# First norm by rows, one root for rows 4 to 7, epsilon on VectorE, fillers on TensorE, and the recurrence put ahead in the scheduler

## The chip, the cores and the metric

One kernel runs on one core of a Trainium2 chip. The metric is the device time of one execution in microseconds (us). The profile gives the times of single instructions on the core's engines: PE (TensorE, matmuls and transposes), PEld (its weight loads), DVE (VectorE), ACT (ScalarE), POOL (GpSimd) and SP (which issues DMAs). "L213" is line 213 of the kernel before; in the rows of the changed kernel's order the line numbers are its own, and the text says which line of the kernel before each one was.

## What is computed

One layer of a decoder: RMSNorm, a gated linear recurrence with eight heads, a squared-ReLU MLP behind a second RMSNorm, and a last RMSNorm. All is float32, 1024 rows by 1024 columns. Cut to what matters here:

```python
def _rmsnorm(x, gain):
    y = x * lax.rsqrt(jnp.mean(x * x, axis=-1, keepdims=True) + NORM_EPS)
    return y * gain

h = _rmsnorm(x, norm_mix)              # the "first norm"
q, f, i, g = jnp.split(h @ w_in, 4, axis=-1)
# per head, over time:  S_t = diag(f_t) S_{t-1} + k_t v_t^T ;  o_t = S_t^T q_t
x = x + (norm(o) * out_norm * silu(g)) @ w_out
x = x + squared_relu_mlp(_rmsnorm(x, norm_mlp))
return _rmsnorm(x, norm_final)
```

## The kernel before

**Products.** A float32 product is made of three matmuls on operands that are split in two parts: `split_mm` (L210 to L213) issues high times high (L211), high times low (L212) and low times high (L213). A splitting is one ACT instruction for the high part and one DVE instruction for the low part: L171 and L172 for the weights `w0a`, `w0c` and so on, L114 and L115 for the sums `ht1` to `ht4`, L313 and L314 for the transposed rows `h0B...`. The first two products (`w0`, `w1`) go plainly, by `plain_pair`; from `w2` on, `pair` uses seven products in place of eight (a Strassen scheme), for which L324 and L334 keep values `R` of the transposed rows.

**First norm.** Eight tiles `x0` to `x7` of 128 rows each are loaded by SP. `stats_1` (L284) makes a row's mean of squares `ss`: on ACT (L290) for even tiles, on DVE (L288) for odd ones. `rstd_of` (L122) then has two POOL instructions: L124 adds epsilon, L125 raises to the power of -0.5. `norm_scale` (L192, DVE) multiplies the tile in place. `transposed` (L196) makes one PSUM bank of four 128x128 transposes (L199, PE), one from each of four row tiles, for one of the eight column blocks kb; so the first bank needs all four tiles. Before them L131 issues 60 transposes of the identity into a bank `warm` that nobody reads.

The first half (`x0` to `x3`) is done at the start. The second half (`x4` to `x7`) is done by a list `hooks`, one entry of which is called ahead of each block kb (three matmuls) of `plain_pair`: statistics, scales, then the banks `tr010` to `tr017` of the second half, each of them in every second entry.

**Recurrence.** For each head `scan_units` (L512) gives a list of units: `small`, `middle`, `leaf(16)`, `big(32)`, `big(64)`, `kt`, and so on, with `None` for an empty place. `pump` (L233) takes one place from the list each time that the projections of the next head have issued 1730 ns of matmuls by its own count (650 per block kb), so that the unit's PE work stands between those matmuls. Between the units stands the chain on DVE: `carry_q`, `carry_k`, `carry_f` (L361, L368, L374) multiply prefixes into `q`, `k`, `f`, for chunks of 1, 2, 4, up to 64; `middle` needs `qe` (L555), `big(32)` and `big(64)` need `q` and `k` after the carries of 16 and 32, `kt` (L624, transposes of `k`) needs the carry of 64, and L596 `tot` stands right behind that carry. `copy_predicated` (L539 to L582) takes the units' results out of PSUM.

**What sets the order.** PE's order is the order of the code, everywhere. Up to L734 (`in_order.close()`), that is until the first half of `w0` and `w1` is done, ACT, DVE and POOL follow the code as well; then a scheduler orders those engines by priorities, until the MLP, where the code's order holds again. All engines run their own queue in order: an instruction that waits holds up what stands behind it.

Of the kernel before, what the change touches and what calls it, by code (L numbers as in the profile page):

```python
# [29 lines left out]
P = 128  # L30
# [13 lines left out]
AHEAD = 6  # L44
WARM = 60


@with_exitstack
def trunk(ctx: ExitStack, tc: tile.TileContext, x, gains, masks, gfin, w_in, w_out, w1, w2, out):
# [72 lines left out]
    def rstd_of(ss, eps, width, tag):  # L122
        r = pool.tile([P, width], F32, name=f"rs_{tag}", tag=f"rs{width}", bufs=8 if width == 1 else 2)
        nc.gpsimd.tensor_scalar(r, ss, eps, None, op0=ALU.add)  # L124
        nc.gpsimd.tensor_tensor(r, r, neghalf[:, :width], ALU.pow)  # L125
        return r


    warm = psum.tile([P, 512], F32, name="warm", tag="d")
    for _ in range(WARM):  # L130
        nc.tensor.transpose(warm[:, :P], ident, ident)  # L131

# [62 lines left out]

    def transposed(which, half, kb, hn, place=None):  # L196
        ps = psum.tile([P, 4, P], F32, name=f"tr{which}{half}{kb}", tag="s")
        for j in range(4):
            nc.tensor.transpose(ps[:, j, :], hn[j][:, kb * P:(kb + 1) * P], ident)  # L199
        name = BLOCKS[half][kb // 4]  # L200
        t = hc[name, kb % 4] = hslot(half if place is None else place, kb, f"h{which}{name}{kb}")
        return ps.rearrange("p a b -> p (a b)"), gn[:, which, kb:kb + 1], t
# [13 lines left out]
    units = []  # L216
    owed = [0.0]
    spacing = [SPACING]

# [3 lines left out]
    def next_unit():  # L223

        u = units[0]
        if isinstance(u, tuple) and u not in complete:
            return False
        units.pop(0)
        if callable(u):
            u()  # L230
        return True
# [17 lines left out]
    with tc.tile_pool(name="scan", bufs=1) as sp:  # L249
# [12 lines left out]
        lb = pool.tile([P, 32], F32, name="lb")  # L262
        gneg, lb = lb[:, 8:16], lb[:, :8]
        lo = pool.tile([P, 8], F32, name="lbe")
# [19 lines left out]
        def stats_1(tb):  # L284

            ss = pool.tile([P, 1], F32, name=f"ss{tb}", tag="ss", bufs=8)
            if tb % 2:
                nc.vector.tensor_tensor_reduce(junk[1], xs[tb], xs[tb], 1.0 / D, 0.0, ALU.mult, ALU.add, ss)  # L288
            else:
                nc.scalar.activation(junk[0], xs[tb], AF.Square, scale=D ** -0.5, accum_out=ss)  # L290
            rs[tb] = rstd_of(ss, EPS, 1, f"n{tb}")

        for tb in range(4):
            stats_1(tb)
        for tb in range(4):
            norm_scale(xs[tb], xs[tb], rs[tb])
        ensure(1)
        nc.gpsimd.memset(Ac, 0.0)
# [10 lines left out]
        def transposes_1(half):  # L309

            def one(kb):
                flat, g, t = transposed(0, half, kb, xs[4 * half:4 * half + 4], 1 - half)
                nc.scalar.activation(t[:, 0], flat, AF.Copy, scale=g)  # L313
# [28 lines left out]
        def scale_1(tb):  # L342
# [4 lines left out]
        hooks += first  # L347
        hooks += [pieces(stats_1, 4, 5), pieces(stats_1, 6, 7), lambda: None, pieces(scale_1, 4, 5),
                  pieces(scale_1, 6, 7)] + [lambda: None] * 7
# [162 lines left out]
        def scan_units(h, tl):  # L512
# [168 lines left out]
            def zt():  # L681

                z = tl["sg"]
                for a in range(2):
# [9 lines left out]

            return (([None] * 5 + [small] + [None] * 3 if h == 0 else [None] * 3 + [small, None, None]) + [middle, None, leaf(16, 7)]
                    + [big(32), big(64), None, kt, ("values", h), vt, kv, None, o_unit, z_unit, None, zt])
# [49 lines left out]
        for h in range(1, NH):  # L746
            tl = heads[h] = {}
            pair(h, tl, 0)
            prefixes(tl)
            units.extend(scan_units(h, tl))  # L750
            if h == NH - 1:
                spacing[0] = LAST_SPACING
            pair(h, tl, 1)
            complete.add(("values", h))
# [437 lines left out]
```

## Time and profile before

| | |
|---|---|
| Time, median of 3 runs | 1164.58 us (1163.2 to 1167.33) |
| Time of the profiled execution | 1162.14 us |
| Its span from first to last instruction | 1160.4 us |
| Around the span | 1.74 us |
| Busy in the span, DVE | 792.7 us (68%) |
| Busy in the span, ACT | 576.3 us (50%) |
| Busy in the span, POOL | 47.6 us (4%) |
| HBM traffic over the span | 123 GB/s |

A row of the timeline reads: start in us from the span's start, length in us, engine, line, operation, output tile <- input tiles, shapes, number of instructions merged into the row, and in brackets how long the engine had stood idle before and what released it. A row of the windows view gives a stretch and its length, then for PE, PEld, DVE, ACT and POOL the busy time and the instructions, then the granted share of TensorE's clock, the DMA engines' share and GB/s. A row of the waits view reads: who waited for whom, us in total, how often, the longest.

### The profile page before, as it was taken

Reading aid. Unit: us, or ns where it says so; the run is one execution under the profiler, and the core shown is the slowest. Engines: PE = TensorE matmul, PEld = TensorE weight load, DVE = VectorE, ACT = ScalarE, POOL = GpSimd, SP = SyncE. Lnnn points to the kernel's source line nnn. Section 1 sums busy time; section 2 is a strip of 40 time slices with the busy share of each in tenths; the row PEclk is TensorE's granted clock in tenths of the full one; section 3 lists DMA queues with packets and bytes.
Section 4 is the critical chain, followed back from the end, with each engine's and each line's share of the span. In section 5 each row is a group of like instructions: output and inputs, shape, how many; then the busy total and the mean of one; then the engine's idle time right before and its main releaser. Section 6 shows DMA issues by size and latency. Waiting matters only on the chain.

```text
span 1160.4 us, 17548 instructions
## 1 busy us (share of the span) xinstructions
PE 1142.0 (98%) x7108; PEld 945.8 (82%) x7108; DVE 792.7 (68%) x1139; ACT 576.3 (50%) x1004; POOL 47.6 (4%) x78
## 2 busy tenths in 40 slices
PE   8999999999999999999999999999999999999997
PEld 7777788887878778888888888888888888888886
DVE  6896868778686876426856645665588756677673
ACT  6646455564645573237545454545453443323552
POOL 3100000000000000010000000000000000000011
PEclk9999999999999999999999999999999999999999
DMA  6111121111112175021245324532797545422331
GB/s 259 37 37 53 41 73 56 46 47 55 44 50 73 56 248 171 19 97 67 91 163 200 122 113 165 199 138 98 272 373 286 186 170 179 148 91 92 127 127 73
DMA packets 43139, 143.38 MB, mean 124 GB/s; under 512 B 4913, under 2 KB 5041, under 8 KB 43057
## 3 DMA queue, kind: packets, MB, share of 16 engines
q1 hardware_dynamic: 42192, 141.05, 34.1%
q8 instruction: 56, 0.92, 0.3%
q10 hardware_dynamic: 864, 1.20, 0.3%
q14 instruction: 27, 0.21, 0.1%
HBM read 100.81 MB, written 41.42 MB: 123 GB/s over the span
## 4 chain that ended last, share of the span: by engine, by line
PE 83%; DVE 12%; ACT 2%; POOL 1%; issue 1%; DMA 1%; POOLq 0%; DVEq 0%; ACTq 0%
PE m2X L213 5%; PE m2X L211 5%; PE m2X L212 5%; PE m1X L212 4%; PE m1X L211 4%; PE m1X L213 4%; PE pX L211 3%; PE pX L213 3%; PE pX L212 3%; PE m2Y L213 3%; PE m2Y L211 3%; PE m2Y L212 2%; PE op L211 2%; PE op L213 2%; PE op L212 2%; DVE k L368 2%
## 5 line engine op out<-in xcount | busy, mean ns | idle before, releaser
L993 ACT ACTIVATE a<-ai 128x1024 fp32r<-128x1024 f32 x56 | 59.0, 1054 | 72.0 <-PE m2X L212 23.6
L994 DVE TENSOR_TENSOR a<-ai,a 128x1024 fp32r<-128x1024 f32 x56 | 68.3, 1220 | 11.5 <-ACT a L993 11.5
L896 ACT ACTIVATE e<-e 128x1024 f32<-128x1024 f32 x21 | 22.3, 1063 | 67.3 <-DVE e L1027 67.3
L211 PE MATMUL op<-wo,zh 128*128 128x512 f32 x128 | 51.0, 398 | 0.0
L213 PE MATMUL op<-wo,zh 128*128 128x512 f32 x128 | 50.0, 391 | 0.0
L212 PE MATMUL op<-wo,zh 128*128 128x512 f32 x128 | 49.8, 389 | 0.0
L151 DVE TENSOR_TENSOR xr<-xr,op 128x512 f32<-128x512 f32 x24 | 16.4, 687 | 44.9 <-PE op L213 44.9
L1054 DVE TENSOR_TENSOR acc<-acc,m2X 128x512 f32<-128x512 f32 x32 | 21.1, 685 | 36.1 <-PE m2X L213 36.0
L361 DVE TENSOR_TENSOR q<-q,f 128x512 f32<-128x512 f32 x56 | 38.6, 689 | 2.0 <-PE lv L609 2.0
L368 DVE TENSOR_TENSOR k<-k,f 128x512 f32<-128x512 f32 x56 | 38.4, 686 | 0.0
L893 ACT ACTIVATE e<-e 128x1024 f32<-128x1024 f32 x32 | 34.0, 1062 | 1.0
L151 DVE TENSOR_TENSOR raw<-raw,raw 128x512 f32<-128x512 f32 x42 | 28.9, 689 | 0.7
L586 ACT ACTIVATE AT<-Ac 32x256 f32<-32x256 f32 x32 | 13.3, 416 | 30.6 <-DVE Ac L582 30.3
L213 PEld LDWEIGHTS op<-wo,zh 128*128 128x128 f32 x128 | 24.0, 188 | 5.2
L211 PEld LDWEIGHTS op<-wo,zh 128*128 128x128 f32 x128 | 24.0, 188 | 4.9
L212 PEld LDWEIGHTS op<-wo,zh 128*128 128x128 f32 x128 | 24.1, 188 | 4.7
L1015 ACT ACTIVATE e<-m1X 128x512 f32<-128x512 f32 x28 | 16.0, 593 | 19.8 <-PE m1X L213 19.8
L124 POOL TENSOR_SCALAR rs_f<-fs 128x1 f32<-128x1 f32 x4 | 2.1, 514 | 577.7 <-ACT ot L1058 577.7
L678 ACT ACTIVATE z<-o,rs_z 128x128 f32<-128x128 f32 x64 | 17.4, 384 | 16.4 <-POOL rs_z L125 16.4
L666 PE MATMUL o<-v,AT 128*128 128x128 f32 x128 | 23.4, 275 | 0.0
L668 PE MATMUL o<-S,q 128*128 128x128 f32 x112 | 21.7, 275 | 0.0
L1054 DVE TENSOR_TENSOR acc<-acc,m2Y 128x512 f32<-128x512 f32 x16 | 10.8, 687 | 15.4 <-PE m2Y L213 13.6
(1721 smaller groups left out, 3731.0 us busy)
## 6 DMA issues: line engine op xcount, KB each, us to landing
raw<-in_w_in SPq DMA_DIRECT2D x32, 512.0 KB, 3.6
ai<-adt SPq DMA_DIRECT2D x32, 512.0 KB, 4.5
adB<-e SPq DMA_DIRECT2D x24, 512.0 KB, 2.6
adt<-t SPq DMA_DIRECT2D x24, 512.0 KB, 4.3
ai<-adB SPq DMA_DIRECT2D x24, 512.0 KB, 4.6
x<-in_x SPq DMA_DIRECT2D x8, 512.0 KB, 7.3
iw<-in_w_out SPq DMA_DIRECT2D x16, 256.0 KB, 3.3
xr<-in_x SPq DMA_DIRECT2D x8, 512.0 KB, 8.2
```

What stands on the lines that cost most here:

```text
L151: nc.vector.tensor_tensor(out_, a, b, ALU.add)
L211: nc.tensor.matmul(ps, lhi, rhi, start=start, stop=False, **more)
L212: nc.tensor.matmul(ps, lhi, rlo, start=False, stop=False, **more)
L213: nc.tensor.matmul(ps, llo, rhi, start=False, stop=stop, **more)
L361: nc.vector.tensor_tensor(qo, qo, te.to_broadcast([P, n, m]), ALU.mult)
L368: nc.vector.tensor_tensor(ke, ke, to.to_broadcast([P, n, m]), ALU.mult)
L666: nc.tensor.matmul(ps[:, j, :], AT[:, c, :], v[:, c, :], start=True, stop=c == 0)
L893: nc.scalar.activation(t, t, AF.Square)
L896: nc.scalar.activation(t, t, AF.Relu, scale=sign)
L993: nc.scalar.activation(hi, x, AF.Copy)
L994: nc.vector.tensor_tensor(lo, x, hi.bitcast(F32), ALU.subtract)
L1054: nc.vector.tensor_tensor(t, t, ps, op)
```

## The change

It has four parts.

1. **Rows.** In the first half of the first norm, the statistics of all four tiles are on ACT. Each tile is scaled as soon as its root is there, and its four transposes go into four banks held open together (`first_banks`). The 60 transposes of the identity become 36 ahead of the first tile, and 6, 6, 6 and 4 behind the transposes of the four tiles.
2. **Epsilon and roots.** In the first norm epsilon is added on DVE. For tiles 4 to 7 the four `ss` stand in one 128x4 tile, so that one DVE addition and one POOL root do for all four. The other norms keep `rstd_of`.
3. **Hooks.** The root has an entry of its own in `hooks`, so all that follows stands one block kb later.
4. **Scheduler.** A unit is recorded with `tc.high_priority(150)`, and with 400 from the second product of the last head on. In the list of head 0 the unit `small` stands one place earlier and the units behind it two places earlier.

```diff
-WARM = 60
+WARM = 36
+WARM_ROW = (6, 6, 6, 4)
...
-    for _ in range(WARM):
-        nc.tensor.transpose(warm[:, :P], ident, ident)
+    def keep_warm(n):
+        for _ in range(n):
+            nc.tensor.transpose(warm[:, :P], ident, ident)
+
+    keep_warm(WARM)
...
+    ahead = [150]
...
         if callable(u):
-            u()
+            with tc.high_priority(ahead[0]):
+                u()
...
-        gneg, lb = lb[:, 8:16], lb[:, :8]
+        gneg, ss4, rs4, lb = lb[:, 8:16], lb[:, 16:20], lb[:, 20:24], lb[:, :8]
...
-            ss = pool.tile([P, 1], F32, name=f"ss{tb}", tag="ss", bufs=8)
-            if tb % 2:
+            ss = ss4[:, tb - 4:tb - 3] if tb >= 4 else pool.tile([P, 1], F32, name=f"ss{tb}", tag="ss", bufs=8)
+            if tb in (5, 7):
...
-            rs[tb] = rstd_of(ss, EPS, 1, f"n{tb}")
-
+            return ss
+
+        def rstd_1(r, ss):
+            nc.vector.tensor_scalar(r, ss, EPS, None, op0=ALU.add)
+            nc.gpsimd.tensor_tensor(r, r, neghalf[:, :r.shape[1]], ALU.pow)
+
+        first_banks = [transpose_bank(0, 0, kb) for kb in range(4)]
         for tb in range(4):
-            stats_1(tb)
-        for tb in range(4):
+            rs[tb] = pool.tile([P, 1], F32, name=f"rs{tb}", tag="rs1", bufs=8)
+            rstd_1(rs[tb], stats_1(tb))
             norm_scale(xs[tb], xs[tb], rs[tb])
+            for kb in range(4):
+                transpose_rows(first_banks[kb], xs, kb, (tb,))
+            keep_warm(WARM_ROW[tb])
...
-        hooks += [pieces(stats_1, 4, 5), pieces(stats_1, 6, 7), lambda: None, pieces(scale_1, 4, 5),
+
+        def rstd_second():
+            rstd_1(rs4, ss4)
+            for i in range(4):
+                rs[4 + i] = rs4[:, i:i + 1]
+
+        hooks += [pieces(stats_1, 4, 5), pieces(stats_1, 6, 7), lambda: None, rstd_second, pieces(scale_1, 4, 5),
...
-            return (([None] * 5 + [small] + [None] * 3 if h == 0 else [None] * 3 + [small, None, None]) + [middle, None, leaf(16, 7)]
+            return (([None] * 4 + [small] + [None] * 2 if h == 0 else [None] * 3 + [small, None, None]) + [middle, None, leaf(16, 7)]
...
             if h == NH - 1:
                 spacing[0] = LAST_SPACING
+                ahead[:] = [400]
```

`transpose_bank` and `transpose_rows` are the two halves of the old `transposed`: the bank, and the transposes of chosen row tiles into it.

**DVE's queue in the first half of the first norm**, before. `ss1` and `ss3` are sums of squares, `rs_n` the roots from POOL, `w0a` the low part of the first weight, `h0B110` the low part of the first transposed block:

```order
L288 ISA junk1_193,ss1_199<-x1_78 128x1024
L288 ISA ss1_199 128x1
L288 ISA junk1_193,ss3_209<-x3_80 128x1024
L288 ISA ss3_209 128x1
L192 TENSOR_SCALAR x0_77<-x0_77,rs_n0_196 128x1024
L192 TENSOR_SCALAR x1_78<-x1_78,rs_n1_201 128x1024
L192 TENSOR_SCALAR x2_79<-x2_79,rs_n2_206 128x1024
L192 TENSOR_SCALAR x3_80<-x3_80,rs_n3_211 128x1024
L172 TENSOR_TENSOR w0a_218<-raw00_163,w0a_218 128x128 x4
L314 SCALAR_TENSOR_TENSOR h0B110_234<-tr000_229,gn_73,h0B110_234 128x512
```

The same place of DVE's queue now (L308 adds epsilon, L197 is the old L192, L177 the old L172, L337 the old L314):

```order
L308 TENSOR_SCALAR rs0_174<-ss0_175 128x1
L197 TENSOR_SCALAR x0_77<-x0_77,rs0_174 128x1024
L308 TENSOR_SCALAR rs1_190<-ss1_191 128x1
L197 TENSOR_SCALAR x1_78<-x1_78,rs1_190 128x1024
L308 TENSOR_SCALAR rs2_206<-ss2_207 128x1
L197 TENSOR_SCALAR x2_79<-x2_79,rs2_206 128x1024
L308 TENSOR_SCALAR rs3_222<-ss3_223 128x1
L197 TENSOR_SCALAR x3_80<-x3_80,rs3_222 128x1024
L177 TENSOR_TENSOR w0a_236<-raw00_139,w0a_236 128x128 x4
L337 SCALAR_TENSOR_TENSOR h0B110_247<-tr000_170,gn_73,h0B110_247 128x512
```

Two statistics have left DVE, four additions of a 128x1 tile have come, and each scale stands directly behind its own addition, with POOL's root between the two.

**DVE's queue in the second half of the first norm**, before (`w1a`, `w1b` and `w1c` are low parts of weights, `qd0` is the first use of a finished product):

```order
L288 ISA junk1_193,ss5_343<-x5_82 128x1024
L288 ISA ss5_343 128x1
L288 ISA junk1_193,ss7_356<-x7_84 128x1024
L288 ISA ss7_356 128x1
L172 TENSOR_TENSOR w1a_367<-raw10_171,w1a_367 128x512
L192 TENSOR_SCALAR x4_81<-x4_81,rs_n4_340 128x1024
L192 TENSOR_SCALAR x5_82<-x5_82,rs_n5_345 128x1024
L192 TENSOR_SCALAR x6_83<-x6_83,rs_n6_353 128x1024
L192 TENSOR_SCALAR x7_84<-x7_84,rs_n7_358 128x1024
L397 SCALAR_TENSOR_TENSOR qd0_384<-qd0_384,qs_188,pp0000_253 128x16x32
L172 TENSOR_TENSOR w1b_396<-raw11_172,w1b_396 128x512
L314 SCALAR_TENSOR_TENSOR h0B120_419<-tr010_414,gn_73,h0B120_419 128x512
```

And now (L302 is the old L288, L116 the old L115; the sums of squares and roots lie in `lb`):

```order
L302 ISA junk1_169,lb_154<-x5_82 128x1024
L302 ISA lb_154 128x1
L116 TENSOR_TENSOR ht33_559<-R11_312,ht33_559 128x512
L302 ISA junk1_169,lb_154<-x7_84 128x1024
L302 ISA lb_154 128x1
L177 TENSOR_TENSOR w1a_349<-raw10_147,w1a_349 128x512
L308 TENSOR_SCALAR lb_154<-lb_154 128x4
L197 TENSOR_SCALAR x4_81<-x4_81,lb_154 128x1024
L197 TENSOR_SCALAR x5_82<-x5_82,lb_154 128x1024
L197 TENSOR_SCALAR x6_83<-x6_83,lb_154 128x1024
L197 TENSOR_SCALAR x7_84<-x7_84,lb_154 128x1024
L426 SCALAR_TENSOR_TENSOR qd0_368<-qd0_368,qs_164,pp0000_256 128x16x32
```

One addition of 128x4 stands ahead of the four scales, and the low part of `ht33`, which stood much later, has come in between the two statistics.

**DVE's queue at the end of head 0's recurrence**, before, from the carry of 16 to `tot` (`raw30` are sums of weights, `w3...` low parts of weights of the next product):

```order
L361 TENSOR_TENSOR q0_383<-q0_383,f0_403 128x32x16
L368 TENSOR_TENSOR k0_402<-k0_402,f0_403 128x32x16
L582 COPY_PREDICATED Ac_177<-mk_74,lv0_16_890 128x256
L374 TENSOR_TENSOR f0_403<-f0_403 128x32
L151 TENSOR_TENSOR raw30_467<-raw30_467,raw31_468 128x512
L361 TENSOR_TENSOR q0_383<-q0_383,f0_403 128x16x32
L368 TENSOR_TENSOR k0_402<-k0_402,f0_403 128x16x32
L172 TENSOR_TENSOR w3s3_1095<-raw30_467,w3s3_1095 128x512
L374 TENSOR_TENSOR f0_403<-f0_403 128x16
L172 TENSOR_TENSOR w3s1_1050<-raw30_467,w3s1_1050 128x512
L361 TENSOR_TENSOR q0_383<-q0_383,f0_403 128x8x64
L368 TENSOR_TENSOR k0_402<-k0_402,f0_403 128x8x64
```

And now, from the carry of 32 on (L390, L397 and L403 are the old L361, L368 and L374, L625 is `tot`, the old L596):

```order
L390 TENSOR_TENSOR q0_367<-q0_367,f0_387 128x16x32
L397 TENSOR_TENSOR k0_386<-k0_386,f0_387 128x16x32
L177 TENSOR_TENSOR w2d_894<-raw21_321,w2d_894 128x512
L403 TENSOR_TENSOR f0_387<-f0_387 128x16
L177 TENSOR_TENSOR w3a_968<-raw30_440,w3a_968 128x512
L390 TENSOR_TENSOR q0_367<-q0_367,f0_387 128x8x64
L397 TENSOR_TENSOR k0_386<-k0_386,f0_387 128x8x64
L625 TENSOR_TENSOR tot0_952<-f0_387 128x8
L177 TENSOR_TENSOR w2s4_891<-raw20_320,w2s4_891 128x512
L177 TENSOR_TENSOR w3b_1000<-raw31_441,w3b_1000 128x512
L156 TENSOR_TENSOR raw30_440<-raw30_440 128x512
L156 TENSOR_TENSOR raw30_440<-raw30_440,raw31_441 128x512
```

Six instructions of 128x512 that stood ahead of `tot` stand behind it now: `w2s4`, `w3b`, two sums `raw30`, `w3s3` and `w3s1`. On PE, `small` of head 0 stands three blocks kb (nine matmuls) earlier, and `kt` one block: the seven transposes of `kt` stood behind the three matmuls of `ht33` and stand ahead of them now. DVE's queue of heads 1 to 6 has not moved, nor has any DMA in SP's queue. ACT's has moved there in one thing: of the four copies L586 of a head, three now stand behind the four copies L612 of `big(32)`. In head 0 the copies L586 and L612 also stand ahead of the evacuation L479 of `pX2` behind `w2s2`, which stood ahead of them.

More of the change, by code (lines that the diff above doesn't have):

```diff
@@ L194, in trunk, with transpose_bank, transpose_rows, transposed @@
     BLOCKS = (("B11", "B21"), ("B12", "B22"))
-    def transposed(which, half, kb, hn, place=None):
-        ps = psum.tile([P, 4, P], F32, name=f"tr{which}{half}{kb}", tag="s")
-        for j in range(4):
+    def transpose_bank(which, half, kb):
+        return psum.tile([P, 4, P], F32, name=f"tr{which}{half}{kb}", tag="s")
+    def transpose_rows(ps, hn, kb, rows):
+        for j in rows:
             nc.tensor.transpose(ps[:, j, :], hn[j][:, kb * P:(kb + 1) * P], ident)
+    def transposed(which, half, kb, hn, place=None, ps=None):
+        if ps is None:
+            ps = transpose_bank(which, half, kb)
+            transpose_rows(ps, hn, kb, range(4))
         name = BLOCKS[half][kb // 4]
@@ L311, in one @@
             def one(kb):
-                flat, g, t = transposed(0, half, kb, xs[4 * half:4 * half + 4], 1 - half)
+                ps = first_banks[kb] if half == 0 and kb < 4 else None
+                flat, g, t = transposed(0, half, kb, xs[4 * half:4 * half + 4], 1 - half, ps)
                 nc.scalar.activation(t[:, 0], flat, AF.Copy, scale=g)
```

## The prediction

> **What bounds the kernel now.** First the page:
>
> ```profile
> span 1160.4 us, 17548 instructions
> PE 1142.0 (98%) x7108; PEld 945.8 (82%) x7108; DVE 792.7 (68%) x1139; ACT 576.3 (50%) x1004; POOL 47.6 (4%) x78
> ```
>
> PE is busy for 98% of the span and no matmul on real data is added or removed, so a change can pay only where PE stands still or runs slowly. The second view is what PE waited for:
>
> ```profile
> PE tr L199 <- DVE x L192: 4.1, 5, 1.2
> PE lv L609 <- DVE k L368: 2.6, 10, 0.7
> PE kt L624 <- DVE tot L596: 1.6, 1, 1.6
> PE lv L561 <- DVE qe L555: 1.3, 1, 1.3
> ```
>
> The first row is the first norm, the third the end of head 0's recurrence, the fourth the last head; the second is spread over all heads. Together they are 9.6 us. The third view is the granted clock, in stretches cut where it changes:
>
> ```profile
> 10.89:14.31 3.42, 1.38 (x9) 0.81 (x8) 2.58 (x5) 0.15 (x2) 3.06 (x5) 1.00 1.03 411
> 14.31:17.72 3.41, 3.41 (x16) 3.12 (x15) 3.06 (x7) 3.08 (x5) 0.00 (x0) 0.50 1.02 406
> ...
> 31.37:34.79 3.42, 1.33 (x7) 0.87 (x6) 2.41 (x4) 1.40 (x3) 1.56 (x3) 1.00 0.01 2
> 34.79:38.20 3.41, 3.41 (x11) 2.73 (x10) 3.23 (x6) 1.74 (x4) 0.00 (x0) 0.50 0.01 2
> ...
> 89.40:92.81 3.41, 1.96 (x13) 1.78 (x14) 2.58 (x6) 1.47 (x4) 0.00 (x0) 1.00 0.02 5
> ```
>
> Behind each stall of the first norm (PE 40% and 39% busy) the clock is 0.50 for 3.41 us. Behind the stall at `kt` (57% busy) no drop follows. So each of the first two stalls is paid twice, and the limit lies between 40% and 57%.
>
> **Part 1, rows.** The identity transposes alone, in two stretches, and then the rows of the chain:
>
> ```profile
> 1.38:7.41 6.03, 6.03 (x28) 6.03 (x29) 1.00 0.91 339
> 7.41:11.12 3.71, 3.70 (x33) 3.46 (x32) 1.00 1.03 417
> ```
>
> ```profile
> 6.04 0.19 ACT L290 ACTIVATION_READ_ACCUMULATOR junk<-x 128x1 f32 x1
> ...
> 8.56 0.57 POOL L125 TENSOR_TENSOR rs_n<-rs_n,neghalf 128x1 f32<-128x1 f32 x1
> ...
> 8.94 1.23 DVE L288 CUSTOM_DVE_ANT_0 junk<-x 128x1024 f32<-128x1024 f32 x1 [1.49 <-DMA x<-in_x]
> ...
> 10.33 1.21 POOL L125 TENSOR_TENSOR rs_n<-rs_n,neghalf 128x1 f32<-128x1 f32 x1
> ...
> 13.09 0.77 DVE L192 TENSOR_SCALAR x<-x,rs_n 128x1024 f32<-128x1024 f32 x1 [0.77 <-POOL rs_n L125]
> ...
> 13.92 2.71 PE L199 MATMUL tr<-ident,x 128*128 128x128 f32 x13 [1.21 <-DVE x L192]
> 14.28 1.36 ACT L313 ACTIVATE h0B<-tr,gn 128x512 fp32r<-128x512 f32 x2 [3.27 <-PE tr L199]
> ```
>
> `x0`'s sum is there at 6.23. Each tile then costs an addition (0.17, as `tot` below, also a few columns on DVE), a root and a scale (0.77), one after the other through DVE, POOL, DVE. The trace has the root at 0.57 and at 1.21, the latter with DVE's scales running beside it, the former with DVE idle. DVE's next instruction now waits for that very root, so I take 0.57 and keep both ends. With 0.04 for hops a tile takes 1.55, and `x3` is scaled at 6.3 + 4 x 1.55 = 12.5, before at 13.86: 1.3 earlier. Its data is in time (there at 8.94), and ACT's sum for it, about as long as DVE's was, ends at 10.2.
>
> The fillers cost nothing if the next tile is later than they are. Of 36, 28 take until 7.41 and eight, at 0.11 each, until 8.3; four transposes and six fillers take 1.1, a tile 1.55. The last four could cost 0.4 in front of the first matmul, which has to wait for ACT anyway.
>
> Behind `x3`, 13 transposes were left; now four. ACT starts 0.36 after the first of them, as from 13.92 to 14.28, so at 12.95, and its four high parts no longer wait for PE. From there on ACT is the one who is late:
>
> ```profile
> 17.25 0.68 ACT L334 ACTIVATE R<-tr,gn 128x512 f32<-128x512 f32 x1
> ...
> 17.82 0.63 ACT L171 ACTIVATE w0c<-raw 128x512 fp32r<-128x512 f32 x1
> ...
> 18.48 0.69 DVE L172 TENSOR_TENSOR w0c<-raw,w0c 128x512 fp32r<-128x512 f32 x1 [0.35 <-ACT w0c L171]
> ...
> 19.78 0.75 DVE L314 SCALAR_TENSOR_TENSOR h0B<-tr,gn,h0B 128x512 fp32r<-128x512 f32 x1 [0.60 <-ACT h0B L313]
> ...
> 26.26 1.22 DVE L288 CUSTOM_DVE_ANT_0 junk<-x 128x1024 f32<-128x1024 f32 x1
> ```
>
> ACT's instructions of this size follow each other every 0.58 (17.25 to 17.82). The first L334 starts at 12.95 + 4 x 0.58 = 15.3 in place of 17.25; behind it stand `w0c`, another L334 and L313, and DVE's wait at 19.78 ends at 17.7: **2.1 earlier**. From 19.78 to 26.26 DVE ran without a gap, so the statistics of `x5` begin at 24.2.
>
> **Parts 2 and 3, root and hook.** The second stall:
>
> ```profile
> 31.14 0.38 PE L199 MATMUL tr<-ident,x 128*128 128x128 f32 x2
> ...
> 33.13 0.75 DVE L192 TENSOR_SCALAR x<-x,rs_n 128x1024 f32<-128x1024 f32 x1 [0.77 <-POOL rs_n L125]
> ...
> 33.80 0.74 DVE L397 SCALAR_TENSOR_TENSOR qd<-qd,qs,pp 128x512 f32<-128x512 f32 x1
> ...
> 34.02 0.48 PE L211 MATMUL pp<-h0B,w1a 128*128 128x512 f32 x1
> ...
> 38.91 0.60 PE L199 MATMUL tr<-ident,x 128*128 128x128 f32 x4
> ...
> 40.74 0.60 PE L199 MATMUL tr<-ident,x 128*128 128x128 f32 x4
> ```
>
> Before, `x6` and `x7` each waited for POOL instructions of their own. Now, from 24.2: two statistics at 1.22, the low part of `ht33` that came in between and that of `w1a` at 0.60 each (two DVE rows below show this step), addition and hops 0.3, root 0.57, three scales at 0.67 (33.13 to 33.80), a last one of 0.75: `x7` is ready at 31.45, before at 33.88. That is **2.4**, and PE's next matmul stands at 31.6 in place of 34.02.
>
> PE came to `tr010` at 31.14; by some 2 earlier now, and by three matmuls later because of the hook, it is there before 30 and still waits for DVE. But those three matmuls, which were still ahead, are done: a period of four transposes and six matmuls is 1.83 (38.91 to 40.74), so a matmul is (1.83 - 0.44) / 6 = 0.23, and three are **0.7**. And the clock: the window at 0.50 held just such a period, 3.41 against 1.83. Those **1.6** go if no drop follows. PE now idles between scales, about 1.0 in a window of 3.4: 70% busy; behind `x3`, fillers, transposes and first matmuls come to some 75%. Both stand above 57%. Start: 2.4 + 0.7 + 1.6 = 4.7.
>
> **Part 4, recurrence.** Head 0:
>
> ```profile
> 55.39 4.91 DVE L115 TENSOR_TENSOR ht<-R,ht 128x512 fp32r<-128x512 f32 x8 [2.06 <-ACT ht L114]
> ...
> 84.72 0.46 DVE L582 COPY_PREDICATED Ac<-mk,lv 128x256 f32<-128x256 uint8 x1
> 84.97 0.46 PE L609 MATMUL lv<-q,k 128*32 128x32 f32 x32 [0.20 <-DVE k L368]
> ...
> 88.81 0.69 DVE L172 TENSOR_TENSOR w3s<-raw,w3s 128x512 fp32r<-128x512 f32 x1 [1.00 <-ACT w3s L171]
> 88.81 0.40 PE L213 MATMUL pX<-ht,w2s 128*128 128x512 f32 x1
> ...
> 90.02 0.68 DVE L368 TENSOR_TENSOR k<-k,f 128x512 f32<-128x512 f32 x1
> 90.62 0.17 DVE L596 TENSOR_TENSOR tot<-f 128x8 f32<-128x8 f32 x1
> ...
> 90.85 0.95 PE L624 MATMUL kt<-ident,k 128*128 128x128 f32 x7 [1.64 <-DVE tot L596]
> ```
>
> Six DVE instructions of 0.60 go behind `tot`, and with them the 1.00 in which one waited for ACT: `tot` ends 4.6 earlier, at 86.2, in before's time. PE would come to `kt` at 89.04 without a wait, less `ht33` (0.8) and the 0.20 at `big(32)`: 88.0. So the stall there goes, 2.04 between two rows that stand 0.23 apart otherwise: 1.8. Next late is `big(32)`: six instructions of 0.60 also leave the queue ahead of L582, so `k` is ready at 81.1, and PE, 15 matmuls earlier, comes at 81.3. I take the 0.20 of there half: **1.9** in all. What is pushed back has room: `w2s4` is split at 86.8, and PE wants it at 89.
>
> Does DVE keep up with a PE that is 4.7 earlier, having gained 2.4 itself? Ahead of head 0 it stood 2.06 waiting for ACT, and `ht33` (0.60) has left that place: 2.4 + 2.06 + 0.6 = 5.1 at most. A tie, with little to spare.
>
> The last head:
>
> ```profile
> 429.08 0.69 DVE L709 TENSOR_TENSOR zh<-iz,zh 128x512 fp32r<-128x512 f32 x1 [1.25 <-ACT zh L708]
> ```
>
> This splitting, which waits for ACT, still stands ahead of the carries; only small copies change places around it: **0.1** of the 1.3. Heads 1 to 6 keep DVE's order, so their waits stay; nothing.
>
> **Sum.** 4.7 + 1.9 + 0.1 = 6.7. The profiled execution took 1162.14 (1160.4 and 1.74 around the span), 2.4 under the median of the three runs, 1164.58. From the median: **1157.9**; from the profiled one 1155.4.
>
> **Rivals.** *The clock falls all the same*, behind `x3` or at `tr010`. For it: the limit was only seen between 40% and 57%. Price: 1.6 at `tr010`; 0.8 behind `x3` (six matmuls at twice 0.23 and four transposes at 0.215 before `tr004` is out, and 17.7 becomes 18.5). Gain 4.3 to 5.9: 1158.7 to 1160.3. The Trainium skill has a rule for this (TensorE: Matmul & The Clock Gate, Part 4): transposes do not count as busy for the clock. By it the fillers hold nothing and the clock falls at both places, 1160.3; by the trace, the forecast. The trace speaks against it: the stretches of Part 1 hold nothing but transposes, 0.215 each up to 7.41 and 0.11 from there, so the clock rose on them alone.
>
> *The root is slow*: 1.21 in place of 0.57, five times, 3.2 more on DVE's chain. `x7` comes at 34.6, the clock falls as before, and little more than head 0 is left: gain 2, 1162.6. Against it: the slow root had long DVE instructions beside it.
>
> *Head 0 gains nothing*: if DVE loses the tie by 2, `big(32)` and `kt` wait as they did: gain 4.8, 1159.8. That the priority does nothing is true already for DVE in six heads.
>
> *Slower.* On ACT the first L586 now stands ahead of L479, the evacuation of `pX2`, and waits for DVE's L582; PE waits for that bank. L582 comes at 81.1, L479 ends, behind L586 and L612, at 85.4, PE wants the bank at 85.6. Each us that L582 is later costs one. To end 3.5 above the median it would have to come some 10 late, at 91, though its old place was 84.72. 1168 or more.
>
> **How the numbers follow.** Forecast 0.58, clock 0.18, no gain in head 0 0.08, slow root 0.12, slower 0.04. A measurement can tell some 0.3% from no change, 3.5: 1161.1 to 1168.1. The first three are faster (0.84), the slow root is within; 0.04 of the forecast goes to within, for the tie. Range: 1154, the profiled run's base with 1.4 for clock drops that the slower runs may have had, to 1162.
>
> **What would show it.** `x3`'s transposes at 12.6; the matmul behind `tr010` at 31.6; clock 1.00 from 7.5 on; no PE wait at `kt`; the `qe` wait of the last head still over 1. Wrong would be: roots over 1 us, a window at 0.50, or a PE wait at `big(32)` over 0.5.

## The result, and the profile after

| | before | changed | ratio (95% interval) |
|---|---|---|---|
| median, first comparison (5 and 5 runs) | 1164.58 us | 1155.50 us | 0.9923 (0.9901 to 0.9944) |
| median, again on another chip (25 and 6 runs) | 1162.84 us | 1157.39 us | 0.9951 (0.9938 to 0.9963) |
| range over both | 1160.20 to 1167.33 | 1154.56 to 1157.76 | |
| profiled execution, first | 1162.14 us | 1156.81 us | |

Faster, by 9.1 us in the first comparison and by 5.4 in the second; 6.7 was forecast. The two profiled executions stand 5.3 apart. The kernel before spreads over 7 us, the changed one over 3, so the medians say less about the parts than the traces do.

The page of the changed kernel:

```profile
span 1155.0 us, 17539 instructions
PE 1138.8 (99%) x7106; PEld 941.4 (82%) x7106; DVE 789.9 (68%) x1140; ACT 577.7 (50%) x1008; POOL 38.6 (3%) x67
```

What PE waits for now (who waited for whom, us in total, times, longest):

```profile
PE lv L590 <- DVE qe L584: 2.6, 1, 2.6
PE lv L638 <- DVE k L397: 1.7, 5, 0.7
...
PE tr L206 <- DVE x L197: 1.2, 4, 0.3
PE tr L206 <- DVE rs L308: 1.2, 3, 0.8
```

The first norm's 4.1 fell to 2.4, the last two rows together: PE waited 1.2 ahead of the transposes of `x3` and at `tr010`, and 1.2 ahead of those of `x0` to `x2`. The row of `kt` is gone. The row of `qe`, the last head, has **doubled**, from 1.3 to 2.6. That was not forecast.

The timeline of the first norm after the change (L197 scales a tile, L206 transposes, L337 is the low part of a transposed block, L309 the root, L223 the first matmul of a block):

```profile
11.52 0.77 DVE L197 TENSOR_SCALAR x<-x,rs 128x1024 f32<-128x1024 f32 x1 [0.66 <-POOL rs L309]
...
12.35 0.66 PE L206 MATMUL tr<-ident,x 128*128 128x128 f32 x4 [0.18 <-DVE x L197]
...
17.43 0.75 DVE L337 SCALAR_TENSOR_TENSOR h0B<-tr,gn,h0B 128x512 fp32r<-128x512 f32 x1 [0.47 <-ACT h0B L336]
...
27.64 1.02 POOL L309 TENSOR_TENSOR lb<-lb,neghalf 128x4 f32<-128x4 f32 x1 [15.10 <-DVE lb L308]
...
28.70 2.74 DVE L197 TENSOR_SCALAR x<-x,lb 128x1024 f32<-128x1024 f32 x4 [1.14 <-POOL lb L309]
...
31.59 0.48 PE L223 MATMUL pp<-h0B,w1a 128*128 128x512 f32 x1
```

`x3` is scaled at 12.29 (forecast 12.5), its transposes start at 12.35 (12.6), DVE's wait for `tr004` ends at 17.43 (17.7), `x7` is ready at 31.44 (31.45) and the matmul behind `tr010` stands at 31.59 (31.6). Once all transposes are done, the same matmul stands 4.70 earlier. In the timeline of before:

```profile
48.43 0.48 PE L211 MATMUL pp<-h0B,w0a 128*128 128x512 f32 x1
```

and in that of the changed kernel:

```profile
43.73 0.47 PE L223 MATMUL pp<-h0B,w0a 128*128 128x512 f32 x1
```

The end of head 0's recurrence, changed:

```profile
81.29 0.17 DVE L625 TENSOR_TENSOR tot<-f 128x8 f32<-128x8 f32 x1
...
83.52 0.93 PE L653 MATMUL kt<-ident,k 128*128 128x128 f32 x7
...
84.98 0.40 PE L223 MATMUL pY<-h0B,w2s 128*128 128x512 f32 x1
```

`tot` ends two us ahead of `kt`, and nothing is waited for. The matmul at 84.98 is the one that stood at 91.56 before: 6.58 earlier, of which head 0 brought 1.9. So far all is as forecast. In the last head, the timeline of before (SPq is a DMA's issue; the first three rows are the store of head 6's `z`, the load of its first half back for `zh06`, and ACT's splittings of `zh`, the first of them that of `zh06`):

```profile
420.99 0.99 SPq L692 DMA_DIRECT2D zd<-sg  x2
424.86 0.32 SPq L718 DMA_DIRECT2D iz<-zd  x1
428.41 1.68 ACT L708 ACTIVATE zh<-iz 128x512 fp32r<-128x512 f32 x3 [1.39 <-DMA iz<-zd]
...
433.24 0.39 PE L213 MATMUL op<-wo,zh 128*128 128x512 f32 x1
434.93 0.46 PE L561 MATMUL lv<-qe,k 128*32 128x48 f32 x25 [1.30 <-DVE qe L555]
```

and of the changed kernel:

```profile
414.37 0.98 SPq L721 DMA_DIRECT2D zd<-sg  x2
418.64 0.32 SPq L747 DMA_DIRECT2D iz<-zd  x1
423.28 1.68 ACT L737 ACTIVATE zh<-iz 128x512 fp32r<-128x512 f32 x3 [2.89 <-DMA iz<-zd]
423.94 0.69 DVE L738 TENSOR_TENSOR zh<-iz,zh 128x512 fp32r<-128x512 f32 x1 [2.54 <-ACT zh L737]
...
426.63 0.39 PE L225 MATMUL op<-wo,zh 128*128 128x512 f32 x1
429.64 0.55 PE L590 MATMUL lv<-qe,k 128*32 128x48 f32 x33 [2.62 <-DVE qe L584]
```

The store is issued 6.62 earlier and PE is 6.61 earlier, but the data is back only 5.13 earlier: the way through DRAM, from the store's issue to ACT's splitting, took 8.9 in place of 7.4. On DVE the low part of `zh06` (423.94) stands ahead of the carries and waits for ACT, so `qe` is late too, and 1.3 of the 6.6 are lost.

### The profile page after: what moved, and what is told of

Same layout as the page of the kernel before. It is cut to its first block, busy times and chain, and to the rows that moved or that the text cites. A ratio compares the mean times of both kernels' runs of the same rounds, so it can differ in the third digit from the quotient of the medians.

```text
span 1155.0 us, 17539 instructions
## 1 busy us (share of the span) xinstructions
PE 1138.8 (99%) x7106; PEld 941.4 (82%) x7106; DVE 789.9 (68%) x1140; ACT 577.7 (50%) x1008; POOL 38.6 (3%) x67
## 4 chain that ended last, share of the span: by engine, by line
PE 87%; DVE 8%; ACT 2%; DMA 1%; issue 1%; POOL 0%; SPq 0%; POOLq 0%; DVEq 0%; ACTq 0%
PE m2X L224 5%; PE m2X L223 5%; PE m2X L225 5%; PE m1X L225 4%; PE m1X L223 4%; PE m1X L224 4%; PE pX L223 3%; PE pX L225 3%; PE pX L224 3%; PE m2Y L224 3%; PE m2Y L225 3%; PE m2Y L223 3%; PE op L223 2%; PE op L225 2%; PE op L224 2%; PE m1Y L225 2%
## 5 line engine op out<-in xcount | busy, mean ns | idle before, releaser
L223 PE MATMUL op<-wo,zh 128*128 128x512 f32 x128 | 51.0, 399 | 0.0
L390 DVE TENSOR_TENSOR q<-q,f 128x512 f32<-128x512 f32 x56 | 38.4, 686 | 2.1 <-PE lv L638 2.0
L397 DVE TENSOR_TENSOR k<-k,f 128x512 f32<-128x512 f32 x56 | 38.2, 683 | 0.0
L223 PEld LDWEIGHTS op<-wo,zh 128*128 128x128 f32 x128 | 24.0, 188 | 4.8
L125 POOL TENSOR_SCALAR rs_f<-fs 128x1 f32<-128x1 f32 x4 | 2.0, 512 | 577.7 <-ACT ot L1088 577.7
```

Source lines behind the costliest of these rows:

```text
L223: nc.tensor.matmul(ps, lhi, rhi, start=start, stop=False, **more)
L390: nc.vector.tensor_tensor(qo, qo, te.to_broadcast([P, n, m]), ALU.mult)
L397: nc.vector.tensor_tensor(ke, ke, to.to_broadcast([P, n, m]), ALU.mult)
```

## The experiments

Twelve runs on three chips, each group beside runs of the kernel before on its chip. "Spans" are those of all executions of a kernel.

| run | median us | before | ratio (95% interval) | spans |
|---|---|---|---|---|
| e1_before | 1163.34 | 1162.84 | 0.9999 (0.9987 to 1.0012) | 1158.3 to 1163.2 |
| e1_start | 1159.68 | 1162.84 | 0.9971 (0.9960 to 0.9982) | 1157.3 to 1158.8 |
| e1_sched | 1160.61 | 1162.84 | 0.9980 (0.9969 to 0.9991) | 1156.5 to 1161.0 |
| e1_after | 1157.39 | 1162.84 | 0.9951 (0.9938 to 0.9963) | 1154.8 to 1155.8 |
| e2_direct | 1154.66 | 1162.07 | 0.9937 (0.9925 to 0.9949) | 1152.7 to 1153.0 |
| e2_list | 1158.12 | 1162.07 | 0.9962 (0.9949 to 0.9976) | 1153.9 to 1156.7 |
| e2_prio | 1158.51 | 1162.07 | 0.9967 (0.9955 to 0.9979) | 1154.7 to 1157.8 |
| e2_nofill | 1156.68 | 1162.07 | 0.9954 (0.9940 to 0.9968) | 1153.3 to 1156.7 |
| e3_oldstart | 1159.02 | 1163.73 | 0.9959 (0.9943 to 0.9974) | 1156.0 to 1157.6 |
| e3_onehook | 1156.15 | 1163.73 | 0.9940 (0.9922 to 0.9957) | 1153.3 to 1155.5 |
| e3_roots | 1153.96 | 1163.73 | 0.9920 (0.9903 to 0.9937) | 1152.0 to 1152.3 |
| e3_epspool | 1154.87 | 1163.73 | 0.9929 (0.9912 to 0.9945) | 1153.0 to 1153.3 |

### The two halves of the change, and both kernels again

**e1_before** is the kernel before, unchanged.

> The kernel before once more, to learn what its runs differ by. Theory: the clock is decided in windows of 3.41 us whose phase differs from one execution to the next, so the three long stalls (behind x0 to x3, at tr010, at kt) cost a half-clock window in some executions and none in others; then the profile shows drops at one to three of these places and no others, the spans lie between 1159 and 1165 us, and the longer ones have the lower mean clock. Rival: the runs differ by something else (DMAs); then the drops stand at the same two places and the mean clock is 0.996 whatever the span.

Its windows view, cut where the clock changes (columns as in the part on the profile before):

```profile
29.42:32.83 3.41, 1.25 (x7) 0.66 (x5) 1.88 (x3) 1.68 (x3) 2.49 (x4) 1.00 0.00 0
32.83:36.24 3.41, 3.23 (x9) 2.55 (x10) 3.38 (x7) 1.21 (x2) 0.00 (x0) 0.50 0.02 5
...
432.19:435.60 3.41, 1.43 (x68) 1.11 (x67) 3.41 (x10) 0.99 (x2) 0.00 (x0) 1.00 1.01 401
435.60:439.01 3.41, 3.41 (x10) 2.64 (x9) 3.41 (x10) 1.26 (x2) 0.00 (x0) 0.50 0.51 188
```

This time the clock fell at `tr010` and in the last head, and not behind `x0` to `x3`. The theory holds in that windows of the same length fell elsewhere; it missed the last head as a place, and the `kt` stall did not make the clock fall here either. The longer executions have the lower mean clock, as the theory has it: 0.997 at a span of 1158.3, 0.995 at 1163.2.

**e1_start** is the changed kernel without the scheduler's part:

```diff
-            with tc.high_priority(ahead[0]):
+            if True:
                 u()
...
-            return (([None] * 4 + [small] + [None] * 2 if h == 0 ...
+            return (([None] * 5 + [small] + [None] * 3 if h == 0 ...
```

> The start of the change alone (rows, epsilon and one root, hook, unused transposes), the scheduler and head 0's list as before. Theory (my sum): 4.7 us less than the profiled execution before, PE's matmul behind tr010 at 31.6 us, no half clock between 7.5 us and the end; the stall at kt of 1.8 us stays, the qe wait of the last head becomes 1.3 to 2.6 us. Span 1155.7 to 1157. Rival (the parts overlap, so that what the start gains is lost again at kt): the stall at kt grows by 2 or more and the span is 1158 or more.

What its PE waited for:

```profile
PE lv L590 <- DVE qe L584: 3.5, 1, 3.5
PE lv L638 <- DVE k L397: 2.2, 9, 0.7
PE kt L653 <- DVE tot L625: 1.6, 1, 1.6
```

The stall at `kt` neither grew nor shrank, so nothing of the start is lost there. The clock was full from 5.7 to 432.3. The span of the profiled execution, 1158.8, lies above what was expected, and so do the others, 1157.3 to 1158.2. Three of the eight are over the rival's 1158, but in the profile it is by another wait: that for `qe` is 3.5, more than the 2.6 allowed for, and a window of half clock follows it.

**e1_sched** is the kernel before with that part alone:

```diff
+    ahead = [150]
...
         if callable(u):
-            u()
+            with tc.high_priority(ahead[0]):
+                u()
...
-            return (([None] * 5 + [small] + [None] * 3 if h == 0 ...
+            return (([None] * 4 + [small] + [None] * 2 if h == 0 ...
...
                 spacing[0] = LAST_SPACING
+                ahead[:] = [400]
```

> The scheduler's part alone (priority 150 and 400, head 0's list), the start as before. Theory: half clock behind x0 to x3 and at tr010 as before, no PE wait at kt, 1.8 to 1.9 us gained in head 0, up to 1.3 us of it given back in the last head, where the low part of zh waits for a load of z that head 6 has only just stored: span 1158.5 to 1159.8. Rival (priority 400 alone lengthens the qe wait): the last head's wait is 2.6 us here too although PE is only 1.9 us earlier.

No wait at `kt`; the `qe` wait is 3.0. That is the rival's sign, a wait as long as the changed kernel's, but not its cause: without any priorities the wait was 3.5 in e1_start and 2.7 in e2_list below. The clock did not fall behind `x3` or at `tr010`, though PE stood there as before (windows view):

```profile
29.14:32.55 3.41, 1.78 (x9) 1.11 (x7) 1.85 (x4) 2.21 (x4) 2.92 (x5) 1.00 0.00 0
...
428.50:431.91 3.41, 1.02 (x5) 0.52 (x3) 3.41 (x10) 1.34 (x3) 0.00 (x0) 1.00 1.03 420
431.91:435.32 3.41, 2.79 (x67) 2.51 (x68) 3.41 (x9) 1.21 (x3) 0.00 (x0) 0.50 0.93 352
```

The window's edge at 29.14 left matmuls on both sides of the stall in it (52% busy), where before the window from 31.37 held 39%. It fell in the last head instead, for two windows. The span, 1160.1, is above what was expected for that reason.

**e1_after** is the changed kernel, unchanged.

> The changed kernel once more. Theory: the load of zd for zh06 lands 8 to 9 us after head 6's store whatever else happens, so the qe wait of the last head is again 2 to 3 us; full clock from the start on; span 1152.8 to 1156. Rival (the load was late by chance in the first profile): the qe wait is 1.3 us and the span 1153.5 or less.

The `qe` wait was 2.5, and a window at half clock, which was not expected, stood behind it, from 429.57. So the changed kernel's wait was long in a second profile too. The halves add up, 0.9971 x 0.9980 = 0.9951, the ratio of both together, but each interval is over 2 us wide, so the medians can't show a loss of 1 us between them.

### What holds the last head, and what each edit does

**e2_direct** splits `zh06` from the tile in which head 6's `z` was made, in place of loading it again:

```diff
                 elif m == "s3":
-                    add(e, e, p_)
+                    add(e, e, p_); (h, j) == (last, 1) and keep_z()
...
-                "s1": ("w", 0, range(4, last), ("m10", "m11")), "s3": ("z", 0, range(last - 1, last), ("m0",))}
+                "s1": ("w", 0, range(4, last), ("m10", "m11"))}
+        def keep_z(): pass_unit(last - 1, "sg"); zh[0, last - 1] = place("z", 0, last - 1); split_value(zh[0, last - 1], heads[last - 1]["sg"][:, HALF[0]])
```

> The changed kernel, but the half of head 6's z that was stored and loaded again for zh06 is split straight from the tile sg6 (the store stays, one load goes). Theory (the qe wait of the last head hangs on this round trip through DRAM): the wait of 2.5 to 2.7 us falls under 0.5, the half clock behind it goes too, span 1152 to 1153.5, some 3 us less than the changed kernel. Rival (DVE is late there with or without the load, by the carries and copies of its own): the wait stays over 1.5 us and the span at 1154.5 to 1156.

Its timeline in the last head:

```profile
418.49 0.69 DVE L738 TENSOR_TENSOR zh<-sg,zh 128x512 fp32r<-128x512 f32 x1
...
426.75 0.69 DVE L584 TENSOR_TENSOR qe<-q,f 128x512 f32<-128x512 f32 x1
...
427.59 0.89 PE L590 MATMUL lv<-qe,k 128*32 128x48 f32 x64 [0.24 <-DVE qe L584]
```

DVE splits `zh06` five us earlier, PE goes on 2.05 earlier, having waited 0.24, and the clock stays full. All spans lie within 0.3 us. So the wait hung on the reload. (The splitting also stands earlier in ACT's and DVE's queues here, which it could not while it waited for the load; the two weren't separated.) Across the nine profiles with the reload, the way from the store's issue to the splitting and the wait at `qe` go together:

| | before | e1_before | e1_start | e1_sched | e1_after | changed | e2_list | e2_prio | e2_nofill |
|---|---|---|---|---|---|---|---|---|---|
| store to splitting, us | 7.42 | 8.11 | 9.69 | 9.30 | 8.78 | 8.91 | 8.82 | 8.78 | 8.12 |
| PE's wait at `qe`, us | 1.3 | 2.0 | 3.5 | 3.0 | 2.5 | 2.6 | 2.7 | 2.5 | 1.8 |

The wait is the way less 6.1 to 6.3 in every one of them. The store itself comes earlier when PE does; it is the way's length that differs. The kernel before has 7.4 and 8.1, the changed one 8.8 and 8.9, and the longest, 9.3 and 9.7, are those of the two halves. So the table doesn't show that the change lengthens the way, nor that it doesn't. What makes it 7.4 once and 9.7 another time stays open; the loads of `xr` and `w_out` run beside it, and taking them away wasn't tried.

**e2_list** is the changed kernel with `if True:` in place of `with tc.high_priority(ahead[0]):`.

> The changed kernel without the priorities (units recorded as before; head 0's list and the start as changed). Theory (the list does the work, the priority next to nothing): PE meets no wait at kt, span within 0.6 us of the changed kernel. Rival (the priority carries head 0 or the last head): a PE wait at kt or big(32) of 1 us or more, or a qe wait 1 us longer than 2.6, and the span 1 to 2 us longer.

The profiled span is 1155.6, with no PE wait at `kt` or at head 0's `big(32)`, and the `qe` wait is 2.7. In the trace the priorities bring nothing that shows. The medians can't say more: the changed kernel didn't run on this chip, and the spans of the two overlap.

**e2_prio** keeps the priorities and takes back head 0's list (`[None] * 5 + [small] + [None] * 3`).

> The changed kernel with head 0's list as it was before (priorities and start as changed). Theory (the list does the work): DVE has six 128x512 instructions ahead of tot again, PE waits 1.6 to 2 us at kt, span 1.5 to 2 us longer than the changed kernel, 1156.5 to 1158. Rival (the priority alone would do): no wait at kt over 0.5 us and a span within 0.5 us of the changed kernel.

Its timeline at the end of head 0:

```profile
85.84 0.17 DVE L625 TENSOR_TENSOR tot<-f 128x8 f32<-128x8 f32 x1
...
86.07 0.95 PE L653 MATMUL kt<-ident,k 128*128 128x128 f32 x7 [1.50 <-DVE tot L625]
```

The wait is back: head 0's gain is the list's. In the changed kernel the list places `small` three blocks kb earlier, so that DVE has the chain's instructions in hand before the splittings of the next weights.

**e2_nofill** is the changed kernel with `WARM_ROW = (0, 0, 0, 0)`.

> The changed kernel without the 22 unused transposes between the rows (the 36 ahead stay). Theory (transposes count for the clock): PE is busy under 45% of a window between 7.5 and 13 us, so a window of 3.41 us at half clock follows there in most executions; it costs 0.2 us on x3's last transposes and up to 0.8 us at x7, span 1155 to 1156.5. Rival 1 (transposes do not count for the clock, so the fillers hold nothing): the granted clock and the span are those of the changed kernel. Rival 2 (the first matmul and ACT are the late ones whatever the clock): the clock falls and the span does not change.

Its windows behind `x3`:

```profile
9.25:12.66 3.41, 1.43 (x9) 0.96 (x10) 2.08 (x6) 1.80 (x6) 2.08 (x4) 1.00 1.03 416
12.66:16.07 3.41, 3.27 (x9) 2.08 (x10) 3.18 (x8) 3.07 (x6) 0.08 (x1) 0.50 1.02 407
```

The clock fell, as the theory has it, and `tr010` came 0.4 later than in the changed kernel; 0.2 of that was there before the clock fell (`x3` was scaled at 12.49 in place of 12.29). The windows of the changed kernel at the same place, and with its two longest stalls:

```profile
7.99:11.40 3.41, 3.08 (x25) 2.60 (x26) 1.63 (x4) 2.72 (x8) 1.55 (x3) 1.00 1.03 417
...
28.47:31.88 3.41, 2.34 (x10) 1.24 (x9) 3.18 (x5) 1.25 (x4) 0.20 (x1) 1.00 0.01 2
427.83:431.24 3.41, 1.60 (x67) 1.45 (x68) 3.41 (x10) 0.65 (x2) 0.00 (x0) 1.00 1.02 398
```

From 7.99 to 11.40 PE did nothing but transposes and kept its full clock. The Trainium skill (TensorE: Matmul & The Clock Gate, Part 4) does not count transposes as busy for the clock in the way of other matmuls; these two runs speak against that. So the first rival is wrong on the clock. In the time the fillers don't show, and what they are worth stays open: the spans overlap those of the changed kernel, which ran on other chips, and in this profile a shorter way through DRAM (8.1) made up for the 0.4.

### The start by itself, on a quiet last head

With e2_direct as base, whose spans lie within 0.3 us, small terms can be told apart. **e3_oldstart** is e1_sched with the edit of e2_direct, so the base with the old start.

> The kernel with zh06 split straight from sg6 (e2_direct), but with the start as before the change. Theory (what the start wins stays won once the qe wait no longer takes part of it back, and the two stalls of the old start draw half-clock windows by chance): 3.1 us more than e2_direct where no window falls at tr010, 4.7 where one does; median 1157.8 to 1160, spread 2 us or more against 0.3 of e2_direct. Rival (the start is worth 3.2, as its run alone against the kernel before would have it, and the give-back in the last head is only apparent): 1157.8 and a spread under 1.

Its spans are 1156.0 to 1157.6, those of e2_direct (on another chip) 1152.7 to 1153.0. The lowest is 3.1 above 1152.9, the highest 4.7. Four lie at 1156.0 to 1156.6 with a mean clock of 0.997, five at 1157.2 to 1157.6 with 0.995 to 0.996. In the one profile, of the second group, at 1157.5, the clock fell behind `x3` and at `tr010`; that the first group had a drop less is inferred from its mean clock. So the start is worth what was forecast, and some 1.6 of it looks drawn by chance. The spread, 1.6, was expected at 2 or more.

**e3_onehook** gives the root no entry of its own:

```diff
-        hooks += [pieces(stats_1, 4, 5), pieces(stats_1, 6, 7), lambda: None, rstd_second, pieces(scale_1, 4, 5),
+        hooks += [pieces(stats_1, 4, 5), pieces(stats_1, 6, 7), rstd_second, pieces(scale_1, 4, 5),
```

> e2_direct with the root for rows 4 to 7 in the empty entry of the list instead of an entry of its own, so that the banks tr010 to tr017 come one block kb earlier. Theory (x7 sets the end of the stall, and the three matmuls that the entry puts ahead of it are won): x7 is scaled at the same time, PE waits 0.7 us longer there, 0.5 to 0.9 us more in all, about 1155.3. Rival (the end is set by ACT's and DVE's parts of those banks behind it, so an earlier bank is no loss): within 0.3 us of 1154.7.

The matmul behind `tr010` stands at 31.57, as in e2_direct, with three matmuls fewer done. (The root began 0.4 earlier, at 27.26, but took 1.39 beside DVE's low part of `w1a`.) The span of the profile, 1153.6, is 0.7 over that of e2_direct; three of the six executions lie there (1153.3 to 1153.6), the other three at 1155.1 to 1155.5 with a lower mean clock (0.997 against 0.998). So the entry won 0.7. That it also saves some executions a drop, by filling PE's window, is inferred: the three longer ones have no profile, and one window of 3.41 us at half clock would lower the mean clock by 0.0015, which a difference of 0.001 fits but doesn't prove.

**e3_roots** takes a root for each tile:

```diff
-        def rstd_second():
-            rstd_1(rs4, ss4)
-            for i in range(4):
-                rs[4 + i] = rs4[:, i:i + 1]
+        def rstd_second(*which):
+            for i in which:
+                rs[4 + i] = rs4[:, i:i + 1]
+                rstd_1(rs[4 + i], ss4[:, i:i + 1])
...
-        hooks += [pieces(stats_1, 4, 5), pieces(stats_1, 6, 7), lambda: None, rstd_second, ...
+        hooks += [pieces(stats_1, 4, 5), lambda: (rstd_second(0, 1), stats_1(6), stats_1(7)), lambda: None, lambda: rstd_second(2, 3), ...
```

> e2_direct with a root of each row tile 4 to 7 in place of one for all: additions and roots of x4 and x5 between the two statistics on DVE, those of x6 and x7 behind them. Theory (the common root, 1.02 us, stands alone on the path while DVE waits 1.14): the first scale starts at 27.6 in place of 28.7, x7 comes 1.0 earlier, the matmul behind tr010 at 30.5 in place of 31.6, about 1153.7. Rival 1 (DVE then loses the tie in head 0, or something behind is late): same time within 0.3. Rival 2 (roots beside DVE's long instructions take 1.2 us each and x6 and x7 wait for them): x7 at 31 or later, gain under 0.5.

POOL's timeline in the second half of the first norm:

```profile
25.26 2.12 POOL L309 TENSOR_TENSOR lb<-lb,neghalf 128x1 f32<-128x1 f32 x2 [12.74 <-DVE lb L308]
27.73 2.17 POOL L309 TENSOR_TENSOR lb<-lb,neghalf 128x1 f32<-128x1 f32 x2 [0.35 <-DVE lb L308]
```

DVE's and PE's:

```profile
27.63 3.06 DVE L197 TENSOR_SCALAR x<-x,lb 128x1024 f32<-128x1024 f32 x4
...
30.82 0.48 PE L223 MATMUL pp<-h0B,w1a 128*128 128x512 f32 x1
```

The first scale starts at 27.63, as expected, but the roots of `x6` and `x7` run beside DVE's scales and take 1.1 each (2.17 for the two), so the four scales take 3.06 in place of 2.74 and the matmul comes 0.75 earlier, not 1.1. The median is 1153.96, 0.7 under e2_direct (on another chip), spans 0.7 lower. Four roots, two of them out of the way in time, beat the common one. With the reload gone as well, this kernel takes 0.9920 (0.9903 to 0.9937) of the time of the kernel before; its spans, 1152.0 to 1152.3, lie under all eleven of the changed kernel (1152.8 to 1156.0, on other chips).

**e3_epspool** adds epsilon on POOL again (`nc.gpsimd.tensor_scalar` in `rstd_1`).

> e2_direct with epsilon of the first norm added on POOL again (rows, common root and all else as changed). Theory (POOL's addition took 0.22 beside an idle DVE and 0.8 to 1.26 beside a busy one, and it would stand ahead of the root on the path): x3 is scaled at 13.3 to 13.8 in place of 12.3, x7 0.2 to 1.0 later, 0.3 to 1.5 us more in all, 1155 to 1156.2. Rival (the addition runs on POOL while DVE scales the tile before, so the rows come faster than now, every 1.3 us or less): x3 at 12.0 or earlier and a time of 1154.7 or less.

Its timeline at `x3`:

```profile
10.17 0.78 POOL L308 TENSOR_SCALAR rs<-ss 128x1 f32<-128x1 f32 x1
11.03 0.57 POOL L309 TENSOR_TENSOR rs<-rs,neghalf 128x1 f32<-128x1 f32 x1
...
11.63 0.77 DVE L197 TENSOR_SCALAR x<-x,rs 128x1024 f32<-128x1024 f32 x1 [0.77 <-POOL rs L309]
```

Both were wrong. The addition takes 0.78 beside DVE's scale of the tile before, but it stands beside it, off the path: `x3` is scaled at 12.4, 0.1 later than with epsilon on DVE. At rows 4 to 7 the addition (0.53) makes the first scale 0.2 later, 28.85. In all 0.2 (1154.87 against 1154.66, spans 0.3 higher): the move of epsilon to DVE is worth next to nothing here.

## Why the prediction came out as it did

**Rows, hook, windows: right.** Start 4.7, measured 4.70 in the pair of profiles. The steps landed within 0.3 us of their times. That `x7` landed at 31.44 against 31.45 is luck: the statistics of `x5` began at 23.91, 0.3 ahead of the forecast, and the root took 0.45 more than was summed.

**The root: mis-sized.** "Root 0.57" was taken from 128x1; the root of 128x4 took 1.02. The trace of before had a nearer row: roots of 128x8 in the heads take 1.67 (L125, median of eight). A straight line from 0.57 for one column to 1.67 for eight gives 1.04 for four. By the prediction's own sign, "roots over 1 us", this step was wrong, if barely. The rival of the slow root was thus half true, but it was paid once and not five times: the four roots of the first half took 0.55 each.

**Clock: the mechanism right, its size no constant.** At `tr010` PE was busy for 69% of the window (70% was forecast), and the clock held. But 1.6 was counted as if every execution of before paid it. The windows' edges lie differently in each execution: of four profiles with the old start two dropped at both places, one at `tr010` alone, one at neither. The changed start kept its clock in all nine profiles that have the fillers, and the spans of e3_oldstart fit the rest: 3.1 over e2_direct in its lowest execution, some 4.6 in the profiled one with both drops. The kernel before owes much of its spread to the clock: beside e3_oldstart its shortest execution, 1157.1, had a mean clock of 0.999 and its longest, 1165.2, one of 0.992.

**Head 0: right**, 1.9 of 1.9, and the list is what does it. That priority moves little was said only for heads 1 to 6; it holds for head 0 too.

**Last head: the step that failed.** "0.1 of the 1.3": the prediction saw that the splitting of `zh06` stands ahead of the carries and waits for ACT, but took its time to move along with PE. It hangs on a store and a load through DRAM. The store did move along, by 6.62; the way behind it took 7.4 us in the profile of before, the shortest of nine, and 8.9 in that of the changed kernel. The term was -1.3, not +0.1. So 4.7 + 1.9 - 1.3 = 5.3, which is what lies between the two profiled executions. How much of the 1.3 belongs to the change and how much to that one short way stays open: in the second profile of the kernel before the wait was 2.0, and against that one only 0.6 would have been lost.

**The sum against the medians.** 1157.9 stood on a median of three runs of a kernel that spreads over 7 us. The first comparison measured 9.1 and the second 5.4; the forecast ratio, 1157.9 / 1164.58 = 0.9943, lies in both intervals. That the other figure, 1155.4 from the profiled execution, stands so near the first median of 1155.50 is luck: the changed kernel's profiled execution took 1156.81. Neither median alone would show which term was off. Of the other rivals none came: no drop behind `x3` or at `tr010`, no lost tie in head 0 (`tot` at 81.46, forecast 86.2 - 4.7 = 81.5), no PE wait for the bank of `pX2`.

## What to carry to other kernels

When everything ahead of a wait moves, ask what the wait hangs on: a round trip through DRAM had another length in each profile here (7.4 to 9.7 us), so one profile's wait is no base for a forecast. A stall's cost has a second part that comes by chance where it empties a clock window, so take the base of a forecast from several profiles. Unused transposes kept the clock up through such a window, though no gain in time was shown for them here. Before several small operations are made one, look for a row with more columns: here the common root took twice as long as a single one, and the single ones could be done ahead of time.

## What the runs showed of the hardware

**In these profiles the clock is decided in fixed windows of 3.41 us, and the limit is sharp.** Full clock began at 4.28 to 7.48 us after the first instruction in fourteen profiles, and changes came only at multiples of 3.41 from there. In a window at full clock that held a stall, either PE was busy for 3% to 45%, and the next one was at half clock, or for 47% and more, and it was at full; no profile had it otherwise. Back to full it takes more: the window at half clock from 431.91 in e1_sched (82% busy, shown above) was followed by another, those of 93% and more by full clock. The two nearest: 1.60 of 3.41 in the changed kernel (427.83, above), no drop, and in e2_prio, a drop:

```profile
429.51:432.92 3.41, 1.54 (x67) 1.41 (x68) 3.41 (x10) 0.71 (x2) 0.00 (x0) 1.00 1.01 386
432.92:436.33 3.41, 3.41 (x10) 2.64 (x9) 3.41 (x10) 2.52 (x4) 0.00 (x0) 0.50 0.34 130
```

Ends of matmuls are modelled, so the limit, between 45% and 47%, is one of the profile's busy time and not of the hardware's own count. The Trainium skill (TensorE: Matmul & The Clock Gate, Part 1) states a free-running window of 3413 ns, which these runs bear out, and a fall after at least one idle window; here a window that was busy for 45% was enough.

**POOL's root grows with the columns, and beside some instructions of DVE**: 0.55 for 128x1 and 1.02 for 128x4 while DVE waited, 1.66 for 128x8 (L126, the roots of the heads), and 1.06 to 1.09 for 128x1 (two roots' time halved, e3_roots) beside DVE's statistics and scales of 128x1024. Not every instruction of DVE does that: in the kernel before the root at 25.19 took 0.57 beside the low parts of `h0B`, and those of 128x8 took 1.67 with a sum of 128x512 beside them (209.07) and with DVE idle (467.77). Which ones do wasn't tried.
